# The entry of a hybrid trunk's feed-forward blocks, written out step by step

## The chip, the cores and the metric

One Trainium2 chip, one core. The metric is the device time of one execution of the whole program in microseconds (us); the profile is one such execution. Engines are named as in the profile: PE (matrix multiplication), PEld (its weight load), DVE (vector engine), ACT (activation engine), POOL (GpSimd), SP (the queue that issues most DMAs). DVE, ACT, POOL and SP each take their instructions in the order in which they were issued.

## The reference, cut to what matters

The program computes one inference step of a two-layer trunk on 640 rows (128 context rows and 512 latent rows) of 1024 values: layer 0 mixes tokens by differential attention, layer 1 by a gated linear recurrence, and each is followed by a feed-forward block. What matters here is the step from the mixer's output to the first feed-forward product:

```
xp = xp + mp[2] * op                # residual add, gated; the same for xs
xp = xp + mp[5] * swiglu(adanorm(xp, g_norm_ffn[i], mp[3], mp[4]), w_ffn_in[i], w_ffn_out[i])

adanorm(x, g, shift, scale) = rmsnorm(x, g) * (1.0 + scale) + shift
swiglu(h, w_in, w_out)      = (silu(gate) * up) @ w_out     # gate, up = halves of h @ w_in
```

## The kernel before, in words

Rows lie in five tiles of 128 (t = 0 to 4, `NT`); the feed-forward block takes them as two halves of 320 columns (`HTOK`), so tile 2 lies in both halves. A product in float32 is made of three in a shorter type: each operand is split into a rounded part (`hi`, by ACT) and the rest (`lo`, a subtraction on DVE or POOL), and hi\*hi, hi\*lo and lo\*hi are summed in PSUM. The input product of the feed-forward block runs as a scheme of seven block products (`ffn_in`), except for the first two column groups (`WHOLE`), which are done as plain products by `whole_in` while the sums of blocks that the scheme needs (`sums`) are still being made.

The function `out_and_ffn` holds the entry, once per layer. For each row tile t:

- `last_head(t)` multiplies the last head into the left half of the output projection, and `add_rows` scales the result by the gate and adds it to the residual row (`rtmp`, then `orow`, both on DVE).
- `row_sums(t)` are 24 products (8 steps of 3) for the right half; `close_rows` does the gated add for it (two DVE instructions, the second adds the old row `xc`) and then `unit_rows`: two squares with sums on ACT, three small POOL instructions that make the scale `rs`, and two scaled copies on ACT into `xr`.
- `to_rows(t, eng)` brings the normalised row into the block: eight transposes on PE from `xr` into two PSUM tiles `ntp` (tag `tp`, only two buffers), then for each half of four: a multiplication on DVE into `Hf`, an addition on POOL in place, a rounded copy on ACT (`A1hi`, or `Thi` and `A2hi` for the second half of the columns) and a subtraction on DVE (`A1lo`, `Tlo`, `A2lo`). Half 0 goes through all four before half 1 is multiplied.
- `whole_weights(f, lo_eng)` loads the weights of a column group into two buffers `wr` (three buffers in all) and splits them: `wh` on ACT, `wl` on POOL in three pieces (group 0) or on DVE (group 1).

From `traced["order"] = True` to `traced["order"] = False` the instructions of DVE, ACT and POOL stay in the order of the program; PE does so while `pe["strict"]` holds; SP's loads do so throughout. Outside of that the scheduler chooses. In layer 0 the entry and the block also carry `fill`: a generator of steps (`take(fill)`) that compute the modulation vectors of later layers, each from two weight tiles `raw` loaded by SP and four small products `psada` on PE.

Of the kernel before, what the change touches and what calls it, by code (L numbers as in the profile page):

```python
# [21 lines left out]
P = 128  # L22
# [37 lines left out]
def trunk_kernel(ctx: ExitStack, tc: tile.TileContext, I, O):  # L60
# [91 lines left out]
    def drain(gen):  # L152
        for _ in gen:
            pass

    def take(gen, n=1):
        for _ in range(n):
            next(gen, None)


    def load_raw(src, dims, slots=None):
        tag, n = next(slots) if slots else ("wr", 3)
        r = wp.tile([P, 1024], F32, name="wr", tag=tag, bufs=n)
        n = int(np.prod(dims))
        v = r[:, :n]
        if len(dims) == 2:
            v = v.rearrange("p (a b) -> p a b", a=dims[0])
        elif len(dims) == 3:
            v = v.rearrange("p (a b c) -> p a b c", a=dims[0], b=dims[1])
        if len(dims) < 3:  # L170
            load(out=v, in_=src)
        elif dims[0] <= dims[1]:
            for a in range(dims[0]):
                load(out=v[:, a], in_=src[:, a])
        else:
            for b in range(dims[1]):
                load(out=v[:, :, b], in_=src[:, :, b])
        return r[:, :n]
# [13 lines left out]
        return out  # L192

    def load_split(src, dims, lo_eng, ordered=False, slots=None):
        r = load_raw(src, dims, slots)
# [1055 lines left out]
    def out_and_ffn(l, oT, w_o, open_rows, gcol, xs, reg, xload):  # L1251
        with ExitStack() as sc:
# [67 lines left out]
            def split_rows(dst, src):  # L1320
                AC.activation(dst[0], src, AF.Copy)
                VE.tensor_tensor(dst[1], src, dst[0], ALU.subtract)

            def to_rows(t, eng):
                g = 0 if t == 0 else 1
                row = xr.pop(t)
                c0, c1 = t * P, min((t + 1) * P, HTOK)
                d0, d1 = max(t * P - HTOK, 0), (t + 1) * P - HTOK
                tps = [turn_x(row, hf) for hf in range(2)]
                halves = [slice(4 * hf, 4 * hf + 4) for hf in range(2)]  # L1330
                for ks, tp in zip(halves, tps):
                    ha = Hf[:, ks, t * P : (t + 1) * P]
                    a, b = (adaC[:, l, w, g, ks].unsqueeze(2).to_broadcast([P, 4, P]) for w in (3, 2))
                    VE.tensor_tensor(ha, tp, a, ALU.mult)
                    eng.tensor_tensor(ha, ha, b, ALU.add)
                    if c0 < c1:
                        split_rows([v[:, ks, c0:c1] for v in A1], Hf[:, ks, c0:c1])
                if d0 < d1:
                    split_rows([v[:, 3, :, d0:d1] for v in S], Hf[:, 0:4, HTOK + d0 : HTOK + d1])
                    split_rows([v[:, :, d0:d1] for v in A22], Hf[:, 4:8, HTOK + d0 : HTOK + d1])  # L1340

            def sums(t):
                c0, c1 = max(t * P - HTOK, 0), (t + 1) * P - HTOK
# [16 lines left out]
            def whole_weights(f, lo_eng):  # L1360
                return [
                    load_split(wi[:, 4 * c : 4 * c + 4, :, f * P : (f + 1) * P], [4, 2, P], lo_eng)
                    for c in range(2)
                ]

            def whole_in(ch, half):
                pss = []
# [111 lines left out]
            def last_head(t):  # L1479
                ps = mm_tile([P, 512], "psr")  # L1480
                drain(row_products(ps, oT, w_o[0], range(H - 1, H), t))
                add_rows(ps, t, 0, gates[0])

            def row_sums(t):
                ps = mm_tile([P, 512], "psr")
# [11 lines left out]
            def close_rows(t, ps, xc):  # L1497
                VE.tensor_tensor(xs[t][:, 512:], ps, gates[1][0 if t == 0 else 1], ALU.mult)
                VE.tensor_tensor(xs[t][:, 512:], xs[t][:, 512:], xc, ALU.add)
                xr[t] = unit_rows(t)  # L1500

            def load_xc(t):
                xc = half_tile("xc")
                nc.sync.dma_start(out=xc, in_=xload(t)[:, 512:])
                return xc

            traced["order"] = True
            for t in range(2):
                last_head(t)
                xc = load_xc(t)  # L1510
                drain(sums_[t][1])
                close_rows(t, sums_[t][0], xc)
            for t in range(2, NT):
                last_head(t)
# [20 lines left out]
            for gi, (f0, f1) in enumerate(FF_GROUPS):  # L1535
                nk = f1 - f0
                if gi == 0:
                    to_rows(NT - 2, PO)
                    first.append(whole_weights(1, VE))
                    sums(2)  # L1540
                    sums(3)
                    take(fill)
                    gus = [whole_in(first[0], 0)]
                    take(fill)
                    to_rows(NT - 1, PO)
                    pe["strict"] = False
# [12 lines left out]
                else:  # L1559
                    open_group(nk)  # L1560
# [168 lines left out]
```

## Time and profile before

| what | us |
|---|---|
| median of three runs (1901.63 to 1903.33) | 1902.78 |
| the profiled execution, its own time | 1901.95 |
| its span in the trace | 1900.1 |
| PE busy in the span | 1806.0 |
| DVE, POOL, ACT busy | 1210.7, 894.7, 807.9 |

The profiled execution is 0.8 us shorter than the median. PE is busy for 95% of the span. The entry of layer 0 lies at about 405 to 500 us of the span, that of layer 1 at about 1402 to 1500 us. In the answers that list instructions a line gives the start in us, the length in us, the engine, the operation with its result and its operands, how many were merged, and in brackets how long the engine had been idle before it and on what it had waited last.

### The profile page before, as it was taken

Reading aid. Unit: us, or ns where it says so; the run is one execution under the profiler, and the core shown is the slowest. Engines: PE = TensorE matmul, PEld = TensorE weight load, DVE = VectorE, ACT = ScalarE, POOL = GpSimd, SP = SyncE. Lnnn points to the kernel's source line nnn. Section 1 sums busy time; section 2 is a strip of 40 time slices with the busy share of each in tenths; the row PEclk is TensorE's granted clock in tenths of the full one; section 3 lists DMA queues with packets and bytes.
Section 4 is the critical chain, followed back from the end, with each engine's and each line's share of the span. In section 5 each row is a group of like instructions: output and inputs, shape, how many; then the busy total and the mean of one; then the engine's idle time right before and its main releaser. Section 6 shows DMA issues by size and latency. Waiting matters only on the chain.

```text
span 1900.1 us, 35139 instructions
## 1 busy us (share of the span) xinstructions
PE 1806.0 (95%) x13759; PEld 1615.4 (85%) x13759; DVE 1210.7 (64%) x1997; ACT 807.9 (43%) x1767; POOL 894.7 (47%) x932
## 2 busy tenths in 40 slices
PE   7999999996999999999999999999987999999997
PEld 5799999775878686898889999999877899998996
DVE  4888887745644444476677666666746665656666
ACT  3566666534424232343543333333334433533443
POOL 3345444323462525267227555555424474575562
PEclk9999999998999999999999999999998999999999
DMA  9512211642465554334332222211231233333331
GB/s 314 162 43 67 60 42 59 202 146 64 144 193 163 173 168 150 122 95 128 111 103 82 60 62 63 62 58 61 80 98 38 78 100 100 96 99 101 99 106 67
DMA packets 228239, 200.57 MB, mean 106 GB/s; under 512 B 11566, under 2 KB 177880, under 8 KB 228073
## 3 DMA queue, kind: packets, MB, share of 16 engines
q1 hardware_dynamic: 227266, 197.73, 33.2%
q8 instruction: 108, 1.77, 0.4%
q10 hardware_dynamic: 806, 0.60, 0.1%
q14 instruction: 59, 0.48, 0.1%
HBM read 190.90 MB, written 7.37 MB: 104 GB/s over the span
## 4 chain that ended last, share of the span: by engine, by line
PE 76%; DVE 10%; DMA 4%; issue 3%; ACT 3%; POOL 3%; SPq 0%; POOLq 0%; DVEq 0%; ACTq 0%
PE psr L96 16%; PE psgu L96 15%; PE psqkv L96 8%; PE psf L96 8%; PE psu L96 7%; PE psvg L96 5%; PE psg L96 3%; PE psada L96 3%; PE pso L96 2%; PE S L96 2%; DVE wl L51 2%; PE pa L96 2%; PE po L96 1%; DVE Q L51 1%; DVE orow L51 1%
## 5 line engine op out<-in xcount | busy, mean ns | idle before, releaser
L51 ACT ACTIVATE wh<-wr 128x1024 fp32r<-128x1024 f32 (+2 forms) x224 | 208.1, 937 | 316.9 <-PE psgu L96 143.6
L51 DVE TENSOR_TENSOR wl<-wr,wh 128x1024 fp32r<-128x1024 f32 (+2 forms) x146 | 184.1, 1266 | 202.8 <-ACT wh L51 200.8
L51 POOL TENSOR_TENSOR wl<-wr,wh 128x341 fp32r<-128x341 f32 (+2 forms) x234 | 217.0, 957 | 168.1 <-ACT wh L51 167.6
L96 PE MATMUL psr<-wh,gT 128*128 128x512 f32 (+1 forms) x888 | 286.7, 394 | 2.2 <-DVE gT L51 1.7
L96 PEld LDWEIGHTS psr<-wh,gT 128*128 128x128 f32 x888 | 165.4, 189 | 49.6 <-issue 8.2
L51 POOL TENSOR_TENSOR xr<-wr 128x512 f32<-128x512 f32 x80 | 121.1, 1515 | 136.6 <-DMA wr<-w_ffn_in 135.5
L51 DVE TENSOR_TENSOR wl<-xr,wh 128x1024 fp32r<-128x1024 f32 x80 | 124.7, 1560 | 94.5 <-ACT wh L51 94.2
L96 PE MATMUL psr<-wl,gT 128*128 128x512 f32 (+1 forms) x444 | 173.5, 391 | 0.0
L51 POOL TENSOR_TENSOR u<-u,p 128x320 f32<-128x320 f32 x40 | 57.6, 1441 | 230.3 <-ACT u L51 230.3
L51 POOL TENSOR_TENSOR orow<-orow,rtmp 128x512 f32<-128x512 f32 x100 | 151.2, 1538 | 26.0 <-DVE rtmp L51 26.0
L51 DVE TENSOR_TENSOR rtmp<-psr,gate 128x512 f32<-128x512 f32 (+1 forms) x131 | 85.5, 679 | 66.6 <-PE psr L96 27.0
L51 POOL TENSOR_TENSOR xr<-wr,xr 128x512 f32<-128x512 f32 x80 | 120.0, 1501 | 15.1 <-DVE wl L51 12.7
L96 PE MATMUL psf<-Thi,wh 128*128 128x320 f32 x384 | 123.7, 322 | 2.9 <-DVE gt L51 2.9
L51 ACT ACTIVATE wh<-xr 128x1024 fp32r<-128x1024 f32 x80 | 84.5, 1059 | 90.3 <-PE psgu L96 46.4
L96 PE MATMUL psgu<-Thi,wh 128*128 128x320 f32 x352 | 110.7, 318 | 11.6 <-ACT p L51 6.0
L96 PE MATMUL psf<-Thi,wl 128*128 128x320 f32 x384 | 118.9, 310 | 0.0
L96 PE MATMUL psf<-Tlo,wh 128*128 128x320 f32 x384 | 118.8, 309 | 0.0
L96 PE MATMUL psqkv<-wh,Thi 128*128 128x384 f32 x320 | 109.2, 357 | 1.4 <-ACT Thi L51 1.4
L96 PE MATMUL psgu<-Tlo,wh 128*128 128x320 f32 x352 | 110.2, 313 | 0.0
L96 PE MATMUL psgu<-Thi,wl 128*128 128x320 f32 x352 | 110.0, 313 | 0.0
L96 PE MATMUL psqkv<-wh,Tlo 128*128 128x384 f32 x320 | 104.5, 340 | 0.5 <-DVE Tlo L51 0.5
L96 PE MATMUL psqkv<-wl,Thi 128*128 128x384 f32 x320 | 103.8, 339 | 0.0
(283 smaller groups left out, 5326.9 us busy)
## 6 DMA issues: line engine op xcount, KB each, us to landing
wr<-w_ffn_in SPq DMA_DIRECT2D x176, 256.0 KB
raw<-w_ada SPq DMA_DIRECT2D x112, 256.0 KB
wr<-w_ffn_out SPq DMA_DIRECT2D x40, 512.0 KB
wr<-w_in_rec SPq DMA_DIRECT2D x64, 256.0 KB
gate<-gdram SPq DMA_DIRECT2D x56, 256.0 KB
wr<-w_qkv_attn SPq DMA_DIRECT2D x64, 192.0 KB
ar<-w_ada SPq DMA_DIRECT2D x24, 512.0 KB
wr<-w_ada SPq DMA_DIRECT2D x16, 512.0 KB
```

Source lines behind the costliest of these rows:

```text
L51: ins = op(*a, **k)
L96: in_order(nc.tensor.matmul(*a, **k))
```

## The change: the entry written out

`to_rows` is taken apart into `turn_rows` (the transposes), `modulate` (multiply both halves, then add to both), and `early_blocks`, `late_blocks` with `hi_of` and `lo_of` (round both, subtract both). The loops of the entry are replaced by a list of calls. The raw weights of group 0 are loaded by a call at the top, those of group 1 before the first `modulate`; their splits are calls of their own. For tiles 3 and 4 `add_rows` follows after the products of all heads, and tile 0 is turned after 3 of the 8 steps of `row_sums(2)` instead of 8. The additions of tile 2 move from POOL to DVE. In layer 0 the first three `take(fill)` are gone; one is put ahead of each `put_gT(group, f, 1, ...)`.

```diff
-            def to_rows(t, eng):
...
-                for ks, tp in zip(halves, tps):
-                    ha = Hf[:, ks, t * P : (t + 1) * P]
-                    a, b = (adaC[:, l, w, g, ks].unsqueeze(2).to_broadcast([P, 4, P]) for w in (3, 2))
-                    VE.tensor_tensor(ha, tp, a, ALU.mult)
-                    eng.tensor_tensor(ha, ha, b, ALU.add)
-                    if c0 < c1:
-                        split_rows([v[:, ks, c0:c1] for v in A1], Hf[:, ks, c0:c1])
...
+            def turn_rows(t):
+                row = xr.pop(t)
+                turned[t] = [turn_x(row, hf) for hf in range(2)]
+
+            def modulate(t, eng):
...
+                for ha, tp, c in zip(has, turned.pop(t), a):
+                    VE.tensor_tensor(ha, tp, c, ALU.mult)
+                for ha, c in zip(has, b):
+                    eng.tensor_tensor(ha, ha, c, ALU.add)
...
+            def hi_of(blocks):
+                for dst, src in blocks:
+                    AC.activation(dst[0], src, AF.Copy)
+
+            def lo_of(blocks):
+                for dst, src in blocks:
+                    VE.tensor_tensor(dst[1], src, dst[0], ALU.subtract)
...
-            for t in range(2, NT):
-                last_head(t)
-            first = [whole_weights(0, PO)]
-            for t in range(2, NT):
-                xc = load_xc(t)
-                ps, products = row_sums(t)
-                take(products, (8, 5, 3)[t - 2])
-                to_rows(t - 2, PO)
-                drain(products)
-                close_rows(t, ps, xc)
+            first[0].append(split_raw(w0[0], PO))
+            add_rows(last_head(2), 2, 0, gates[0])
+            pss = [last_head(t) for t in range(3, NT)]
+            xc = load_xc(2)
+            ps2, products = row_sums(2)
+            take(products, 3)
+            turn_rows(0)
+            for ps, t in zip(pss, range(3, NT)):
+                add_rows(ps, t, 0, gates[0])
+            first[0].append(split_raw(w0[1], PO))
+            w1 = whole_weights(1)
+            modulate(0, PO)
+            hi_of(early_blocks(0))
+            take(products, 4)
+            turn_rows(1)
+            drain(products)
+            close_rows(2, ps2, xc)
+            xc = load_xc(3)
+            modulate(1, PO)
+            lo_of(early_blocks(0))
+            hi_of(early_blocks(1))
+            lo_of(early_blocks(1))
+            ps3, products = row_sums(3)
+            drain(products)
+            close_rows(3, ps3, xc)
+            xc = load_xc(4)
+            ps4, products = row_sums(4)
+            take(products, 2)
+            turn_rows(2)
+            modulate(2, VE)
+            hi_of(early_blocks(2))
+            lo_of(early_blocks(2))
+            drain(products)
+            hi_of(late_blocks(2))
+            close_rows(4, ps4, xc)
+            lo_of(late_blocks(2))
...
-                    to_rows(NT - 2, PO)
-                    first.append(whole_weights(1, VE))
+                    turn_rows(3)
+                    modulate(3, PO)
+                    first.append([split_raw(w, VE) for w in w1])
+                    hi_of(late_blocks(3))
+                    lo_of(late_blocks(3))
                     sums(2)
                     sums(3)
-                    take(fill)
                     gus = [whole_in(first[0], 0)]
-                    take(fill)
-                    to_rows(NT - 1, PO)
-                    pe["strict"] = False
+                    turn_rows(4)
+                    modulate(4, PO)
+                    hi_of(late_blocks(4))
+                    lo_of(late_blocks(4))
                     sums(4)
                     weights = ffn_weights(WHOLE)
                     traced["order"] = False
+                    pe["strict"] = False
                     gus.append(whole_in(first[1], 0))
-                    take(fill)
                     open_group(nk)
...
                     for f in range(WHOLE):
+                        take(fill)
                         put_gT(group, f, 1, whole_in(first[f], 1))
                         take(fill)
```

How the instructions stand, DVE at the entry of layer 1, in the kernel before (from the multiplication of tile 0; `orow` is the gated add of a row's right half):

```order
L51 TENSOR_TENSOR Hf<-ntp,adaC 128x4x128
L51 TENSOR_TENSOR A1lo<-Hf,A1hi 128x4x128
L51 TENSOR_TENSOR Hf<-ntp,adaC 128x4x128
L51 TENSOR_TENSOR A1lo<-Hf,A1hi 128x4x128
L51 TENSOR_TENSOR orow<-psr,gate 128x512
L51 TENSOR_TENSOR orow<-orow,xc 128x512
L51 TENSOR_TENSOR Hf<-ntp,adaC 128x4x128
```

The same place in the changed kernel:

```order
L51 TENSOR_TENSOR Hf<-ntp,adaC 128x4x128 x2
L51 TENSOR_TENSOR orow<-psr,gate 128x512
L51 TENSOR_TENSOR orow<-orow,xc 128x512
L51 TENSOR_TENSOR Hf<-ntp,adaC 128x4x128 x2
L51 TENSOR_TENSOR A1lo<-Hf,A1hi 128x4x128 x4
L51 TENSOR_TENSOR orow<-psr,gate 128x512
L51 TENSOR_TENSOR orow<-orow,xc 128x512
```

The subtractions `A1lo` of tiles 0 and 1 moved behind the multiplications of both tiles and behind the closing of tile 2.

ACT, between the scaled copies of tile 4 and the block sums (the same in both layers), as one piece of the difference; `wh` are the rounded weights of group 1, `Thi` and `A2hi` the rounded blocks of tile 3:

```order
 L51 ACTIVATE xr,nss<-orow 128x512 x2
 L51 ACTIVATE xr<-orow,rs 128x512 x2
+L51 ACTIVATE wh<-wr 128x1024 x2
 L51 ACTIVATE Thi<-Hf 128x4x128
 L51 ACTIVATE A2hi<-Hf 128x4x128
-L51 ACTIVATE wh<-wr 128x1024 x2
 L51 ACTIVATE Thi<-Hf 128x8x64
```

The two weight roundings moved ahead of the blocks of tile 3. ACT's other rows of the entry and POOL's, except for the two additions of tile 2, stand as before.

PE in layer 0, behind the 48 products of the first `whole_in` (`psgu`), before:

```order
L96 MATMUL psgu<-A1lo,wh 128x320
L96 MATMUL psgu<-A1hi,wl 128x320
L96 MATMUL psada<-raw,cT 32x256 x2
L96 MATMUL psgu<-A1hi,wh 128x320
L96 MATMUL psgu<-A1lo,wh 128x320
```

and now:

```order
L96 MATMUL psgu<-A1lo,wh 128x320
L96 MATMUL psgu<-A1hi,wl 128x320
L99 MATMUL ntp<-ident,xr 128x128 x8
L96 MATMUL psgu<-A1hi,wh 128x320
L96 MATMUL psgu<-A1lo,wh 128x320
```

The transposes of tile 4 stand directly behind the first `whole_in`, and the first `psada` stands some 95 products later. SP's order in the entry of layer 1 is unchanged; in that of layer 0 it is so up to the eighth `wr<-w_ffn_in` behind the rows `xc`, where four loads of `raw` now follow in place of eight.

## Rows read from the trace of the kernel before

**Rows 1.** PE's waits in 368 to 520 us (layer 0): for what, us, times, longest.

```profile
PE psada L96 <- DMA raw<-w_ada: 9.4, 2, 8.7
PE ntp L99 <- DVE Hf L51: 8.9, 3, 5.5
```

**Rows 2.** PE's waits in 1340 to 1520 us (layer 1), the same columns.

```profile
PE ntp L99 <- DVE Hf L51: 8.9, 3, 5.6
PE psgu L96 <- ACT Thi L51: 5.2, 1, 5.2
PE psgu L96 <- ACT p L51: 3.3, 1, 3.3
```

**Rows 3.** Timeline of PE, layer 1: start, length, instruction, idle before.

```profile
1405.08 0.47 PE L96 MATMUL psr<-wh,Thi 128*128 128x512 f32 x1
...
1415.40 1.04 PE L99 MATMUL ntp<-ident,xr 128*128 128x128 f32 x8
...
1425.86 1.09 PE L99 MATMUL ntp<-ident,xr 128*128 128x128 f32 x4 [5.56 <-DVE Hf L51]
...
1444.08 0.62 PE L96 MATMUL psgu<-A1hi,wh 128*128 128x320 f32 x1
...
1452.27 1.03 PE L99 MATMUL ntp<-ident,xr 128*128 128x128 f32 x8
...
1465.99 1.44 PE L96 MATMUL psgu<-Thi,wh 128*128 128x320 f32 x4 [5.17 <-ACT Thi L51]
```

**Rows 4.** Timeline of POOL, layer 1.

```profile
1417.46 5.27 POOL L51 TENSOR_TENSOR wl<-wr,wh 128x341 fp32r<-128x341 f32 x6 [2.40 <-ACT wh L51]
...
1422.69 1.03 POOL L51 TENSOR_TENSOR Hf<-Hf,adaC 128x512 f32<-128x512 f32 x1
```

**Rows 5.** Timeline of ACT, layer 1.

```profile
1412.36 0.61 ACT L51 ACTIVATE xr<-orow 128x512 f32<-128x512 f32 x1
...
1415.10 1.34 ACT L51 ACTIVATE xr<-orow,rs 128x512 f32<-128x512 f32 x2 [1.42 <-POOL rs L51]
...
1416.34 1.99 ACT L51 ACTIVATE wh<-wr 128x1024 fp32r<-128x1024 f32 x2
...
1426.86 0.63 ACT L51 ACTIVATE A1hi<-Hf 128x512 fp32r<-128x512 f32 x1 [2.48 <-POOL Hf L51]
...
1431.52 1.33 ACT L51 ACTIVATE xr<-orow,rs 128x512 f32<-128x512 f32 x2 [1.21 <-POOL rs L51]
```

**Rows 6.** Timeline of DVE, layer 1.

```profile
1416.04 0.69 DVE L51 TENSOR_TENSOR Hf<-ntp,adaC 128x512 f32<-128x512 f32 x1 [0.61 <-PE ntp L99]
...
1424.42 0.69 DVE L51 TENSOR_TENSOR A1lo<-Hf,A1hi 128x512 fp32r<-128x512 f32 x1 [7.69 <-ACT A1hi L51]
...
1428.85 0.69 DVE L51 TENSOR_TENSOR orow<-orow,xc 128x512 f32<-128x512 f32 x1
...
1452.84 2.35 DVE L51 TENSOR_TENSOR wl<-wr,wh 128x1024 fp32r<-128x1024 f32 x2
...
1455.12 0.87 DVE L51 TENSOR_TENSOR Hf<-Hf 128x256 f32<-128x256 f32 x2
```

**Rows 7.** Timeline of DVE, layer 0.

```profile
418.96 0.69 DVE L51 TENSOR_TENSOR Hf<-ntp,adaC 128x512 f32<-128x512 f32 x1 [0.61 <-PE ntp L99]
...
458.03 0.87 DVE L51 TENSOR_TENSOR Hf<-Hf 128x256 f32<-128x256 f32 x2
...
471.38 1.29 DVE L51 TENSOR_TENSOR Hf<-ntp,adaC 128x512 f32<-128x512 f32 x2 [4.97 <-PE ntp L99]
```

**Rows 8.** Timelines of PE and of SP's queue, layer 0.

```profile
464.23 1.07 PE L96 MATMUL psada<-raw,cT 128*32 128x256 f32 x4 [8.73 <-DMA raw<-w_ada]
...
459.09 18.91 SPq L91 DMA_DIRECT2D raw<-w_ada  x8
```

**Rows 9.** Timeline of POOL, layer 1, later: the first column differences of weights.

```profile
1471.80 3.99 POOL L51 TENSOR_TENSOR xr<-wr 128x512 f32<-128x512 f32 x2
...
1509.77 1.38 POOL L51 TENSOR_TENSOR xr<-wr 128x512 f32<-128x512 f32 x1 [5.96 <-DMA wr<-w_ffn_in]
```

More of the change, by code (lines that the diff above doesn't have):

```diff
@@ L194, in load_split, with split_raw @@
     def load_split(src, dims, lo_eng, ordered=False, slots=None):
-        r = load_raw(src, dims, slots)
+        return split_raw(load_raw(src, dims, slots), lo_eng, ordered)
+    def split_raw(r, lo_eng, ordered=False):
         n = r.shape[1]
@@ L1322, in split_rows @@
                 VE.tensor_tensor(dst[1], src, dst[0], ALU.subtract)
-            def to_rows(t, eng):
-                g = 0 if t == 0 else 1
-                row = xr.pop(t)
-                c0, c1 = t * P, min((t + 1) * P, HTOK)
-                d0, d1 = max(t * P - HTOK, 0), (t + 1) * P - HTOK
-                tps = [turn_x(row, hf) for hf in range(2)]
-                halves = [slice(4 * hf, 4 * hf + 4) for hf in range(2)]
-                for ks, tp in zip(halves, tps):
-                    ha = Hf[:, ks, t * P : (t + 1) * P]
-                    a, b = (adaC[:, l, w, g, ks].unsqueeze(2).to_broadcast([P, 4, P]) for w in (3, 2))
-                    VE.tensor_tensor(ha, tp, a, ALU.mult)
-                    eng.tensor_tensor(ha, ha, b, ALU.add)
-                    if c0 < c1:
-                        split_rows([v[:, ks, c0:c1] for v in A1], Hf[:, ks, c0:c1])
-                if d0 < d1:
-                    split_rows([v[:, 3, :, d0:d1] for v in S], Hf[:, 0:4, HTOK + d0 : HTOK + d1])
-                    split_rows([v[:, :, d0:d1] for v in A22], Hf[:, 4:8, HTOK + d0 : HTOK + d1])
+            HALVES = [slice(4 * hf, 4 * hf + 4) for hf in range(2)]
@@ new lines, in out_and_ffn @@
+            turned = {}
+            def turn_rows(t):
+                row = xr.pop(t)
+                turned[t] = [turn_x(row, hf) for hf in range(2)]
+            def modulate(t, eng):
+                g = 0 if t == 0 else 1
+                has = [Hf[:, ks, t * P : (t + 1) * P] for ks in HALVES]
+                a, b = ([adaC[:, l, w, g, ks].unsqueeze(2).to_broadcast([P, 4, P]) for ks in HALVES] for w in (3, 2))
+                for ha, tp, c in zip(has, turned.pop(t), a):
+                    VE.tensor_tensor(ha, tp, c, ALU.mult)
+                for ha, c in zip(has, b):
+                    eng.tensor_tensor(ha, ha, c, ALU.add)
@@ new lines, in early_blocks, with late_blocks @@
+            def early_blocks(t):
+                c0, c1 = t * P, min((t + 1) * P, HTOK)
+                return [([v[:, ks, c0:c1] for v in A1], Hf[:, ks, c0:c1]) for ks in HALVES] if c0 < c1 else []
+            def late_blocks(t):
+                c0, c1 = max(t * P - HTOK, 0), (t + 1) * P - HTOK
+                if c0 >= c1:
+                    return []
+                dsts = [v[:, 3, :, c0:c1] for v in S], [v[:, :, c0:c1] for v in A22]
+                return [(dst, Hf[:, ks, HTOK + c0 : HTOK + c1]) for dst, ks in zip(dsts, HALVES)]
@@ L1358, in put_late_sums @@
                     split_rows([v[:, 3, :, c0:c1] for v in S], s4)
[L1360 to L1364, printed above, removed]
             def whole_in(ch, half):
@@ L1481, in last_head @@
                 drain(row_products(ps, oT, w_o[0], range(H - 1, H), t))
-                add_rows(ps, t, 0, gates[0])
+                return ps
             def row_sums(t):
@@ L1505, in load_xc, with whole_weights @@
                 return xc
+            def whole_weights(f):
+                return [load_raw(wi[:, 4 * c : 4 * c + 4, :, f * P : (f + 1) * P], [4, 2, P]) for c in range(2)]
             traced["order"] = True
+            w0 = whole_weights(0)
+            first = [[]]
             for t in range(2):
-                last_head(t)
+                ps = last_head(t)
                 xc = load_xc(t)
                 drain(sums_[t][1])
+                add_rows(ps, t, 0, gates[0])
                 close_rows(t, sums_[t][0], xc)
-            for t in range(2, NT):
-                last_head(t)
-            first = [whole_weights(0, PO)]
-            for t in range(2, NT):
-                xc = load_xc(t)
-                ps, products = row_sums(t)
-                take(products, (8, 5, 3)[t - 2])
-                to_rows(t - 2, PO)
-                drain(products)
-                close_rows(t, ps, xc)
+            first[0].append(split_raw(w0[0], PO))
[6 more added lines that the diff above has]
+            for ps, t in zip(pss, range(3, NT)):
+                add_rows(ps, t, 0, gates[0])
+            first[0].append(split_raw(w0[1], PO))
[25 more added lines that the diff above has]
+            lo_of(late_blocks(2))
             fill = iter(())
```

## The prediction

> **What bounds the kernel now.** I first read PE's waits, since PE is busy for 95% of the span: outside the two entries they are short, inside they are the largest of the trace. In layer 1 PE waits 8.9 us in three pieces before transposes, because DVE has not yet emptied the two `ntp` buffers, 5.2 us for the rounded blocks `Thi` of tile 4, and 3.3 us for an eviction `p` at the start of the first `ffn_in` [rows 2]. In layer 0 it waits the same 8.9 us, and 9.4 us for `raw`, the weights of a `fill` step, 8.7 of them in one piece [rows 1, 8]. So the question is what those waits hang on. The timelines say: on a chain that hardly touches PE. POOL makes `wl` of group 0 in six pieces, from 1417.46 to 1422.73, and only then adds to the first half of tile 0 [rows 4]; DVE meanwhile sits idle 7.69 us before the first `A1lo` [rows 6], and since the multiplication of half 1 stands behind that `A1lo`, PE's second four transposes of tile 1 wait 5.56 us [rows 3]. After that the same round (DVE, POOL, ACT, DVE) goes on tile by tile, with the closing of the next tile in its middle, up to the block sums (first `Hf<-Hf` on DVE, 1455.12) [rows 6]. From these on DVE has almost no gaps until the `p` of the first `ffn_in`.
>
> **Two identical layers.** The first multiplication of tile 0 is at 418.96 in layer 0 and 1416.04 in layer 1, a distance of 997.08; the block sums start at 458.03 and 1455.12, a distance of 997.09 [rows 6, 7]. So I work out layer 1 and carry it over; only what comes behind the sums differs. All times below are on layer 1's clock.
>
> **What the change does to the chain.** It removes no instruction of the entry but reorders DVE and PE; ACT and POOL keep their rows, save for the additions of tile 2 and one swap on ACT. The start of the chain therefore stays: tile 1 closes before the split as it does now, ACT rounds `wr` at 1416.34 [rows 5], POOL ends `wl` at 1422.73. I put 0.3 us on top for DVE work that now runs beside it, so 1423.0. From there, with the durations of the rows:
> - POOL adds both halves of tile 0 without a gap, since both are multiplied: 2 x 1.03 gives 1425.1 [rows 4]. ACT rounds the second, 0.63: 1425.7 [rows 5].
> - ACT stands in order, so the squares of tile 2 come only now. From the first square to the first scaled copy is 15.10 - 12.36 = 2.74 us, the two copies 1.34 [rows 5]: `xr` of tile 2 is there at 1429.8.
> - POOL, free of `rs` at 1428.4, adds tile 1: 1430.5; ACT rounds, 0.63: 1431.1; DVE subtracts, 0.69: 1431.8; DVE closes tile 3 with two instructions of 0.69: 1433.2.
> - From the end of such a closing to the first copy is 1431.52 - 1429.54 = 1.98 us [rows 5, 6]: 1435.2, and 1436.5 with the copies. ACT and DVE then finish the early half of tile 2 (half-wide instructions, together 1.0, an estimate from half of 0.63 and of 0.69): 1437.5. Here the first `whole_in` can start on PE; now it starts at 1444.08 [rows 3].
> - DVE closes tile 4: 1438.9; its late half of tile 2 and the multiplications of tile 3, 0.7 and 1.4: 1441.0. ACT copies tile 4 from 1440.9 to 1442.2, rounds the weights, 1.99 [rows 5]: 1444.2, and then tile 3, 2 x 0.63: 1445.5. DVE's two `wl` take 2.35 [rows 6], the second from 1444.2: 1445.4; the two subtractions of tile 3, 1.4: 1446.9.
>
> The block sums start at 1446.9 in place of 1455.12, which is **8.2 us earlier**. What follows (sums, tile 4, `Thi`) has the same rows on DVE, ACT and POOL, so PE's second half of `whole_in` starts at 1457.8 in place of 1465.99 [rows 3], provided PE is done with the two first halves: 1437.5, twice 8.19 (48 products, 1444.08 to 1452.27 [rows 3]) and the transposes give about 1454.9. It is, and waits some 3 us still.
>
> **What PE still waits for.** PE's transposes of tile 0 come after 30 products in place of 45; at 10.32 / 45 = 0.229 us each [rows 3] that is 1412.0, just when `xr` of tile 0 is made, ahead of ACT's square at 1412.36 [rows 5], so that costs at most 0.5. `ntp` is then emptied at once and the three waits of 8.9 us in all go [rows 2]. What is late next is `xr` of tile 2: PE has done 12 products, the transposes of tile 1 and 33 products by about 1425 and stands until 1429.8, close to 5 us. That wait is new, but it lies inside the chain above and is not added to it.
>
> **Behind the sums, layer 0.** There the multiplication of tile 4 waits 4.97 us for PE's transposes [rows 7], because these stand behind a `psada` that waited 8.73 us for `raw` [rows 8]. The changed order on PE puts them ahead of every `fill` step, as in layer 1, where no such wait is. So layer 0 gains 8.2 + 5.0 = **13.2 us**. The `raw` loads sit on SP behind eight weight loads, the last of which waits for `wl` of group 1; that ends at 1445.4 - 997.1 = 448.3, against 458.0 now (1452.84 + 2.35 - 997.1 = 458.1) [rows 6], so `raw` is issued about 449 in place of 459.09 [rows 8] while its first use on PE moves behind two `whole_in`, to about 468. Landing takes about 5 us (459.09 to 464.23 [rows 8]): it is covered by some 14 us.
>
> **The parts with small or no price.** Loading `w0` at the top issues nothing new, since SP's order in the entry is as before: 0; if it delayed `xc` of tile 2, used at about 1419, it would cost what it is late. The swap on ACT is inside the sum. The two additions of tile 2 on DVE cost 1.4 us there, in a stretch where DVE waits for ACT's rounding of tile 2: 0, at worst 1.4 per layer. One `fill` step less before the first `ffn_in` only moves it: 0, or its own 1 us [rows 8]. At the start of `ffn_in`, DVE's `p` and ACT's eviction for it no longer stand behind a `gT`; that may shorten the 3.3 us [rows 2] by up to 1.6 in each layer, and I take 0, since DVE's `wl` there is no earlier than the chain.
>
> **The sum.** 13.2 + 8.2 = 21.4 us off the profiled 1901.95 gives 1880.6; the median stands 0.8 above that execution, so **1881.4, rounded to 1881**.
>
> **Where the Trainium skill speaks against it.** POOL ran two weight differences at 3.99 / 2 = 2.00 us each while DVE was at work, and a like one at 1.38 later [rows 9]. The Trainium skill (GPSIMD Engine Reference, Specifications) says that GpSimd shares its SBUF interfaces with VectorE, with contention from DVE instructions that have two SBUF inputs. The trace agrees by these two rows. By that rule the new DVE work beside `wl` would slow the chain's first link; the price, from rows, is the second rival.
>
> **The rivals.**
> - *All waits go.* If the chain has slack that I don't see, the three longest waits of layer 1 and the two of layer 0 vanish: 17.4 + 18.3 = 35.7 us [rows 1, 2], giving 1867. Against it: ACT still runs the squares of tile 2 behind tile 0's rounding. 12%.
> - *POOL slows beside DVE.* If `wl` stretches as 2.00 to 1.38, 5.27 becomes 7.6, 2.4 us per layer, 4.8 in all: 1886. Of DVE's instructions in that stretch only one of four reads two SBUF tiles, which is why I took 0.3. 16%.
> - *It does not do what it says.* If the second round keeps the sums where they are because tile 4's closing, not tile 0's, sets them, then only the 5 us of layer 0 are left: 1898. The row at 1428.85 speaks against it, since the closing stands late only because of the `A1lo` before it. 5%.
> - *Slower: `fill` starves in layer 0.* The steps shift by one slot through the whole layer and the scheduler there lays PE out anew. Each late `raw` can cost what one cost in the entry, 8.73 us [rows 8]. It decides at the third: three take 26.2 and leave 1881 + 26 = 1907. For it: the loads share SP with the weights. Against it: the loads are issued about 10 us earlier, and each step's weights are asked for one step ahead. 5%.
>
> **How the numbers follow.** My forecast has 62%. Its own range is 1873 to 1889: down by 3.2 (both `p`) and a part of the waits after it, up by 2.8 for tile 2's additions, 0.6 for tile 0's transposes and some latency per link. With the rivals on both sides, 1866 to 1891 leaves out about 2 in 10. What this kernel's measurement can tell from no change is 0.2%, or 3.8 us. Faster: 62 + 12 + 16 + 3 of the third rival = 93%, less 2 for overlooked mishaps, 91%; the same 3%; slower 6%.
>
> **What would show it.** Right: in both layers the block sums start about 31 us after the first multiplication of tile 0 in place of 39.1 (1455.12 - 1416.04); DVE's idle time before the first `A1lo` is spent on tile 1 and the closing of tile 2; PE's waits for `Hf` at `ntp` are nearly gone and one of about 5 us for `xr` stands there; no 8.73 us wait for `raw` in layer 0. Wrong: PE still waiting for `Thi` as long before and the sums at 39 us; a `wl` group on POOL well above 5.3 us; new waits for `raw` after 500 us; or PE without any wait in the entry, which would mean that the chain was not the bound.

## The result and the profile after

| | median us | range us | runs |
|---|---|---|---|
| before | 1902.2 | 1898.9 to 1903.3 | 4 |
| changed | 1886.3 | 1885.1 to 1889.8 | 4 |

The ratio is 0.9922, with a 95% interval of 0.9904 to 0.9941: 15.9 us faster where 21.4 were forecast, and inside the range of 1866 to 1891. The profiled execution took 1889.76 us, its span is 1887.9. It is 3.5 us above the median, and it lost as much ahead of every changed instruction: at 65 us PE's granted clock fell to 0.50 after a wait for modulation weights (last section), and layer 0's entry begins 4.13 us later than in the trace of before (first `rtmp` of tile 0 on DVE at 413.11 against 408.98). Times of layer 0 below are given with these 4.13 taken off, called *adjusted*; layer 1's entry begins 2.14 us earlier than before's, and there 2.14 is added.

PE's waits around the entry of layer 1, in the changed kernel (what PE waited for, us, times, longest):

```profile
PE psgu L96 <- ACT Thi L51: 5.4, 1, 5.4
PE ntp L99 <- ACT xr L51: 5.1, 2, 4.2
PE psgu L96 <- ACT p L51: 1.8, 1, 1.8
...
PE ntp L99 <- DVE Hf L51: 0.3, 1, 0.3
```

Beside [rows 2], the 8.9 us for `Hf` are down to 0.3, the wait for `xr` of tile 2 has come in their place, the one for `Thi` is as long as it was, and the one for `p` has lost 1.5. In layer 0 the wait of 8.7 us for `raw` [rows 1] is gone (372 to 525 us):

```profile
PE psada L96 <- DMA raw<-w_ada: 0.5, 2, 0.2
```

PE's timeline in layer 1 shows where the waits stand (start, length, instruction, idle time before it and what ended it):

```profile
1414.05 1.23 PE L99 MATMUL ntp<-ident,xr 128*128 128x128 f32 x8 [0.28 <-DVE Hf L51]
1427.00 1.97 PE L99 MATMUL ntp<-ident,xr 128*128 128x128 f32 x8 [4.23 <-ACT xr L51]
...
1456.35 1.43 PE L96 MATMUL psgu<-Thi,wh 128*128 128x320 f32 x4 [5.38 <-ACT Thi L51]
```

The last row answers to 1465.99 of [rows 3]: adjusted 1458.49, 7.5 us earlier. DVE, the same stretch:

```profile
1413.22 1.28 DVE L51 TENSOR_TENSOR Hf<-ntp,adaC 128x512 f32<-128x512 f32 x2
...
1417.62 1.28 DVE L51 TENSOR_TENSOR Hf<-ntp,adaC 128x512 f32<-128x512 f32 x2
1422.82 1.69 DVE L51 TENSOR_TENSOR A1lo<-Hf,A1hi 128x512 fp32r<-128x512 f32 x2 [3.93 <-ACT A1hi L51]
...
1432.02 1.28 DVE L51 TENSOR_TENSOR Hf<-Hf,adaC 128x512 f32<-128x512 f32 x2
...
1445.49 0.88 DVE L51 TENSOR_TENSOR Hf<-Hf 128x256 f32<-128x256 f32 x2
```

Tile 1 is multiplied before the first `A1lo`, whose wait is 3.93 us in place of 7.69. From the first multiplication to the block sums it is 32.27 us in place of 39.08 [rows 6]; in layer 0 it is 32.23 (422.41 to 454.64). POOL, where the chain begins:

```profile
1415.33 5.80 POOL L51 TENSOR_TENSOR wl<-wr,wh 128x341 fp32r<-128x341 f32 x6 [2.40 <-PE ntp L99]
1421.08 2.04 POOL L51 TENSOR_TENSOR Hf<-Hf,adaC 128x512 f32<-128x512 f32 x2
...
1425.36 0.19 POOL L51 TENSOR_SCALAR ms<-nss 128x1 f32<-128x1 f32 x1
1425.64 0.55 POOL L51 TENSOR_TENSOR rs<-ms,mhalf 128x1 f32<-128x1 f32 x1
...
1432.02 0.74 POOL L51 TENSOR_SCALAR ms<-nss 128x1 f32<-128x1 f32 x1
1432.84 0.88 POOL L51 TENSOR_TENSOR rs<-ms,mhalf 128x1 f32<-128x1 f32 x1
```

`wl` takes 5.80 us where it took 5.27 [rows 4], and the two small instructions of tile 3 take 1.6 us together where those of tile 2 take 0.7: they run at 1432.02, beside DVE's additions of tile 2.

**Where the rest went.** I follow one instruction of each `ffn_in` of layer 0 on DVE (`u<-u,psu`). In the changed kernel:

```profile
501.74 0.48 DVE L51 TENSOR_TENSOR u<-u,psu 128x320 f32<-128x320 f32 x1
518.23 0.48 DVE L51 TENSOR_TENSOR u<-u,psu 128x320 f32<-128x320 f32 x1
578.96 0.49 DVE L51 TENSOR_TENSOR u<-u,psu 128x320 f32<-128x320 f32 x1 [0.55 <-PE psu L96]
...
934.79 0.48 DVE L51 TENSOR_TENSOR u<-u,psu 128x320 f32<-128x320 f32 x1
```

and in the kernel before:

```profile
511.03 0.48 DVE L51 TENSOR_TENSOR u<-u,psu 128x320 f32<-128x320 f32 x1
530.31 0.47 DVE L51 TENSOR_TENSOR u<-u,psu 128x320 f32<-128x320 f32 x1
576.71 0.48 DVE L51 TENSOR_TENSOR u<-u,psu 128x320 f32<-128x320 f32 x1
...
936.59 0.48 DVE L51 TENSOR_TENSOR u<-u,psu 128x320 f32<-128x320 f32 x1
```

The first comes 9.29 us earlier (adjusted 13.4), the second 12.08, the third 2.25 later. Between the second and the third, where the first `rows_out` stands (the output product of the first group of columns), 14.3 us are lost; the expectations below call this stretch that between the third and fourth `ffn_in`. About 4 come back later, for a reason that was not followed up: at the last of the 20 rows the lead is 1.80, adjusted 5.9. PE at the first `rows_out`, in the changed kernel:

```profile
521.30 0.50 PE L96 MATMUL psr<-wh,gT 128*128 128x512 f32 x1 [1.68 <-ACT gT L51]
523.77 0.73 PE L96 MATMUL psr<-wh,gT 128*128 128x512 f32 x2 [1.27 <-DVE gT L51]
528.05 1.07 PE L96 MATMUL psada<-raw,cT 128*32 128x256 f32 x4 [3.54 <-DMA raw<-w_ada]
```

and the load it waits for on SP's queue:

```profile
522.90 7.05 SPq L91 DMA_DIRECT2D raw<-w_ada  x6
```

The busy times by stretch of 10 us (PE, PEld, DVE, ACT, POOL, granted clock, DMA share, GB/s), changed kernel:

```profile
515.00:525.00 10.00, 6.55 (x38) 5.33 (x36) 7.12 (x10) 4.23 (x7) 3.87 (x4) 1.00 0.48 137
525.00:535.00 10.00, 6.95 (x23) 4.82 (x23) 1.29 (x3) 0.00 (x0) 3.88 (x4) 0.66 0.52 179
```

and before, where PE has no gap at all:

```profile
515.00:525.00 10.00, 10.00 (x62) 7.74 (x61) 3.00 (x4) 3.56 (x8) 1.30 (x1) 1.00 0.48 141
525.00:535.00 10.00, 10.00 (x58) 9.16 (x58) 6.16 (x8) 4.55 (x8) 6.42 (x5) 1.00 0.34 100
```

The order of PE tells why. Before, 11 `fill` steps stand ahead of the first `rows_out`: a set of modulation vectors (ten steps, the first of which only loads) ends in them, the loads of the next set are asked for, its first products stand ahead of the last `psu` (519.19), and behind that `psu` come 45 `psr` in a row. The changed kernel has 10. The set still ends there, but the next set's first products stand 6 `psr` behind the last `psu`, and their `raw` is asked for at 522.90 only, behind six weight loads. The other traces say the same. In every kernel with 10 steps ahead (the changed one and, of those below, fill_minus, l0_only, lo_inline, w1_after, tile2_pool, wl_late), 11.2 to 14.8 us are lost in this stretch and PE waits 3.5 to 5.1 us for `raw` (fill_held, which moves later steps too: 8.1 and 3.1); in every one with 11 (fill_plus, l1_only, fill_wait, wl_late_wait, steps_behind) no more than about 1 us is lost, and that wait is 0.3 us or less.

### The profile page after: what moved, and what is told of

Its sections match the earlier page's. It is cut to its first block, busy times and chain, and to the rows that moved or that the text cites. A ratio compares the mean times of both kernels' runs of the same rounds, so it can differ in the third digit from the quotient of the medians.

```text
span 1887.9 us, 35138 instructions
## 1 busy us (share of the span) xinstructions
PE 1804.6 (96%) x13759; PEld 1612.6 (85%) x13759; DVE 1210.9 (64%) x2001; ACT 807.9 (43%) x1767; POOL 890.9 (47%) x928
## 4 chain that ended last, share of the span: by engine, by line
PE 75%; DVE 9%; POOL 4%; DMA 4%; issue 4%; ACT 3%; SPq 0%; POOLq 0%; DVEq 0%; ACTq 0%
PE psr L96 16%; PE psgu L96 14%; PE psqkv L96 8%; PE psf L96 8%; PE psu L96 7%; PE psvg L96 5%; PE psg L96 3%; PE psada L96 2%; PE pso L96 2%; PE S L96 2%; DVE wl L51 2%; PE pa L96 2%; PE po L96 1%; DVE Q L51 1%; POOL wl L51 1%
## 5 line engine op out<-in xcount | busy, mean ns | idle before, releaser
L96 PE MATMUL psgu<-Thi,wh 128*128 128x320 f32 x352 | 111.7, 320 | 14.8 <-ACT Thi L51 10.8
```

What stands on the lines that cost most here:

```text
L96: in_order(nc.tensor.matmul(*a, **k))
```

## The experiments

Theory A: the chain through POOL, ACT and DVE sets the end of the entry, the change shortened it about as worked out, and what is missing was lost to the moved `fill` step in layer 0. Rival B: POOL's slowing beside DVE took it, in both entries alike. Rivals C and D are named where they are tested. Each group of kernels has its own runs of the kernel before, and the ratio goes by these. Where two kernels of different groups are compared, the difference of their ratios (the changed kernel has 0.9922) stands beside that of their medians: the two can be 3 to 4 us apart.

| kernel | us | ratio to before, 95% interval |
|---|---|---|
| fill_plus | 1882.8 | 0.9886, 0.9865 to 0.9907 |
| fill_minus | 1907.2 | 1.0019, 1.0008 to 1.0031 |
| l1_only | 1889.9 | 0.9932, 0.9909 to 0.9954 |
| l0_only | 1896.0 | 0.9966, 0.9950 to 0.9983 |
| lo_inline | 1895.8 | 0.9970, 0.9954 to 0.9986 |
| w1_after | 1888.1 | 0.9920, 0.9892 to 0.9948 |
| tile2_pool | 1884.1 | 0.9901, 0.9873 to 0.9929 |
| wl_late | 1875.9 | 0.9849, 0.9815 to 0.9883 |
| fill_wait | 1882.1 | 0.9883, 0.9865 to 0.9901 |
| fill_held | 1881.6 | 0.9884, 0.9870 to 0.9898 |
| wl_late_wait | 1869.2 | 0.9824, 0.9810 to 0.9838 |
| steps_behind | 1900.1 | 0.9985, 0.9970 to 0.9999 |

**The step that was dropped, put back (fill_plus) and taken from the kernel before (fill_minus).** On the changed kernel:

```diff
                         take(fill)
+                    take(fill)
                     put_late_sums()
```

> The changed kernel with one more fill step (a product of the modulation weights) directly behind the second put_gT of the entry in layer 0, so that 11 steps in place of 10 stand ahead of the first rows_out, as in the kernel before. Theory A (the engine chain gained what was forecast, and the step that was dropped costs about 7 us between the third and fourth ffn_in of layer 0): PE's order in the first rows_out is again the old one, the waits there for raw and gT go, time 1879 to 1881 against 1886. Rival B (POOL beside DVE in the entries took the missing gain): the entries are the same, so the time stays at 1886, plus or minus 1.

On the kernel before:

```diff
                     gus.append(whole_in(first[1], 0))
-                    take(fill)
                     open_group(nk)
```

> The kernel before with its third fill step of layer 0's entry left out at that place (the steps themselves are all done, one slot later), nothing else: 10 in place of 11 steps ahead of the first rows_out. Theory A: this alone loses what the changed kernel loses there, about 7 us: 1909 against 1902. Rival B: a step that moves costs nothing: 1902, plus or minus 1.5.

fill_minus lost 0.19%, about 4 us by the runs. Its trace loses 14.8 us between the second and the third `ffn_in` of layer 0 and is 6.1 behind at the end of the layer, in a kernel whose entry is otherwise as before. PE there, the same two rows as in the changed kernel:

```profile
529.29 0.50 PE L96 MATMUL psr<-wh,gT 128*128 128x512 f32 x1 [1.68 <-ACT gT L51]
...
536.27 1.07 PE L96 MATMUL psada<-raw,cT 128*32 128x256 f32 x4 [4.86 <-DMA raw<-w_ada]
```

fill_plus has no such loss: 1.0 us between those two `ffn_in`. It gains 3.5 us by the medians, less than expected, and 6.8 by the ratios. It has a late `raw` of its own, 2.2 us at 492 us, with PE's clock at 0.73 in the 5 us from 491, and its lead at the first `ffn_in` is 10.0 us (adjusted by the 3.33 that its own entry begins later) where the changed kernel has 13.4. Rival B expected no change from either kernel, and falls as the main cause; the size is 4 to 7 us by the times.

**One layer at a time (l1_only, l0_only).** Old entry and new in one kernel:

```diff
+            NEW = l == 1
+            if NEW:
+                w0 = whole_weights(0)
...
+            else:
+                for t in range(2):
+                    old_head(t)
```

> The new entry in layer 1 alone, the old one in layer 0. Theory A (layer 1 gains all of the chain, about 10 us; layer 0 gains 13 and loses 7 again in its first rows_out): 1892. Rival B (contention in both entries takes the missing gain alike, so that each has half of 16): 1894. If only layer 0's wait for raw counted: 1902. A and B are told apart more by the trace: in A the block sums of layer 1 stand 31 to 32 us behind the first multiplication of tile 0, and layer 0 is as before.

> The new entry in layer 0 alone (with its order of the fill steps), the old one in layer 1. Theory A: 13 us ahead at the first ffn_in, 6 ahead at the end of layer 0: 1896. Rival B: 1894, and no loss between the third and fourth ffn_in. With layer 1 alone the two gains should add up to the 16 us of the whole change, within 1.5.

Layer 1 alone gives 12.9 us by its ratio, layer 0 alone 6.5. The sum of 19.4 misses the 16 within 1.5 that I expected; the ratios' intervals are 3 to 4 us wide to either side, so it does not disagree with 15.9 either. Rival B wanted equal halves; the traces decide: in l1_only the sums stand 32.3 us behind the first multiplication in layer 1 and 39.1 in layer 0. In l0_only the lead of layer 0 goes from 13.0 us at the second `ffn_in` to 1.3 behind at the third (not adjusted; its entry begins 2.67 later than that of before), and PE waits 4.7 us for `raw` there.

**DVE's order alone undone (lo_inline).**

```diff
+            def old_modulate(t, eng):
...
+                for ks, tp, blk in zip(HALVES, turned.pop(t), early_blocks(t)):
...
+                    VE.tensor_tensor(ha, tp, a, ALU.mult)
+                    eng.tensor_tensor(ha, ha, b, ALU.add)
+                    hi_of([blk])
+                    lo_of([blk])
...
-            modulate(0, PO)
-            hi_of(early_blocks(0))
+            old_modulate(0, PO)
...
-            modulate(1, PO)
-            lo_of(early_blocks(0))
-            hi_of(early_blocks(1))
-            lo_of(early_blocks(1))
+            old_modulate(1, PO)
```

> The changed kernel with tiles 0 and 1 handled half by half again (multiply, add, round, subtract of half 0 before the multiplication of half 1), all else as changed. Theory A (the order multiply both, then the rest, on DVE is what shortens the chain): PE's waits for Hf at ntp come back (5 to 6 us in each layer), the block sums start 36 to 39 us behind the first multiplication of tile 0 in place of 32.2, and the time is 1894 to 1898. Rival C (the gain is that of the swap on ACT, the early loads and the order on PE): sums stay near 32 us, time 1886 to 1888.

The old wait is back, in one piece of 9.0 us in each layer (I had put 5 to 6 on it). This is layer 1, the wait and DVE's first multiplication and first block sum:

```profile
PE ntp L99 <- DVE Hf L51: 9.3, 2, 9.0
...
1410.56 0.68 DVE L51 TENSOR_TENSOR Hf<-ntp,adaC 128x512 f32<-128x512 f32 x1
...
1448.43 0.87 DVE L51 TENSOR_TENSOR Hf<-Hf 128x256 f32<-128x256 f32 x2
```

The sums stand 37.9 us behind the first multiplication in both layers: 5.6 of the 6.8 us that the change took out of this stretch are DVE's order for tiles 0 and 1. 9.5 us are lost by the medians, 9.1 by the ratios. Theory A as expected in the sums and the time; rival C (the swap, the loads, PE's order) is left with the other 1.2.

**The swap on ACT undone (w1_after) and tile 2 on POOL again (tile2_pool).**

```diff
-                    first.append([split_raw(w, VE) for w in w1])
                     hi_of(late_blocks(3))
                     lo_of(late_blocks(3))
+                    first.append([split_raw(w, VE) for w in w1])
```

> The changed kernel with the split of the weights of group 1 behind the rounding and subtracting of tile 3, as before. Theory A: the swap only changes the order at the chain's end; the blocks of tile 3 come 2 us earlier, wl ends later, the sums move by at most 1 us per layer: 1885 to 1888. Rival C: half of the gain or more goes: 1893 or later.

```diff
-            modulate(2, VE)
+            modulate(2, PO)
```

> The changed kernel with the two additions of tile 2 on POOL again. Their 1.28 us leaves DVE, and POOL's rs of tile 3, which took 0.74 and 0.88 us beside them in place of 0.19 and 0.55, should be back at these. Theory A: POOL's two additions take 2.0 us where DVE's took 1.3, so the blocks of tile 2 come about 0.7 later while xr of tile 3 comes 0.9 earlier: sums at 31.3 to 32.5 us, 1885 to 1887. Rival B (contention is what eats the gain): sums 1 us earlier or more in each layer, 1884 or less.

The swap is worth nothing: 1888.1 and sums at 32.20. With tile 2 on POOL the two small instructions of tile 3 are back at 0.19 and 0.55, and the sums come at 31.85, 0.4 earlier:

```profile
1429.95 0.19 POOL L51 TENSOR_SCALAR ms<-nss 128x1 f32<-128x1 f32 x1
1430.22 0.55 POOL L51 TENSOR_TENSOR rs<-ms,mhalf 128x1 f32<-128x1 f32 x1
```

So rival B's mechanism exists, and taking it away is worth 0.4 us per layer here; the 2.2 us between the medians (4.0 between the ratios) are within the spread of the runs.

**POOL's differences out of the chain (wl_late).** The rounding of `w0` stays, POOL's six `wl` go behind `rs` of tile 3, and the loads of group 1 with them:

```diff
-            first[0].append(split_raw(w0[0], PO))
+            his = [split_hi(w0[0])]
...
-            first[0].append(split_raw(w0[1], PO))
-            w1 = whole_weights(1)
+            his.append(split_hi(w0[1]))
...
             close_rows(3, ps3, xc)
             xc = load_xc(4)
+            first[0] = [split_lo(r, hi) for r, hi in zip(w0, his)]
+            w1 = whole_weights(1)
```

> The changed kernel with POOL's six differences wl of group 0 (5.8 us) moved from ahead of the additions of tile 0 to behind rs of tile 3; their rounding on ACT stays. Theory A (the chain through POOL sets the end of the entry): xr of tile 2 comes 5 us earlier, PE's wait for it (4.2) goes, the block sums start 27 to 28.5 us behind the first multiplication in place of 32.2, PE's wait for Thi falls from 5.4 to under 2, and the time is 1875 to 1879. Rival D (DVE and ACT, not POOL, set the end): sums stay within 1 us of 32.2, 1885 to 1887. Against A: rs of tile 4 then stands behind wl, and the weights of group 1 get their slots later; if that decides, 1883 or later.

1875.9 us, 10.4 below the changed kernel (13.9 by the ratios). POOL adds to tile 0 at once, and DVE's sums stand 28.27 us behind the first multiplication in place of 32.27:

```profile
1410.24 2.04 POOL L51 TENSOR_TENSOR Hf<-Hf,adaC 128x512 f32<-128x512 f32 x2 [1.04 <-DVE Hf L51]
...
1424.27 6.10 POOL L51 TENSOR_TENSOR wl<-wr,wh 128x341 fp32r<-128x341 f32 x6
...
1409.48 1.28 DVE L51 TENSOR_TENSOR Hf<-ntp,adaC 128x512 f32<-128x512 f32 x2
...
1437.75 0.88 DVE L51 TENSOR_TENSOR Hf<-Hf 128x256 f32<-128x256 f32 x2
```

The chain is the bound, and POOL was its first link. PE's wait for `xr` of tile 2 is gone, as expected. Not as expected, the one for `Thi` grew to 6.30 us: the chain reaches `Thi` 4.0 us sooner after the first multiplication, but PE arrives 4.9 sooner:

```profile
1418.91 1.03 PE L99 MATMUL ntp<-ident,xr 128*128 128x128 f32 x8
1425.11 1.27 PE L99 MATMUL ntp<-ident,xr 128*128 128x128 f32 x8 [1.07 <-ACT xr L51]
...
1448.62 1.43 PE L96 MATMUL psgu<-Thi,wh 128*128 128x320 f32 x4 [6.30 <-ACT Thi L51]
```

**Where a `fill` step may stand (fill_wait, fill_held, steps_behind).** fill_wait, on the changed kernel, puts the first step's products into PE's wait for `Thi`. To hold them there it also keeps PE's order strict through the second of the two first halves:

```diff
+                    take(fill)
                     gus = [whole_in(first[0], 0)]
...
+                    gus.append(whole_in(first[1], 0))
+                    take(fill)
                     pe["strict"] = False
-                    gus.append(whole_in(first[1], 0))
...
                     for f in range(WHOLE):
-                        take(fill)
+                        if f:
+                            take(fill)
```

> The changed kernel with 11 fill steps ahead of the first rows_out, as fill_plus, but with the loads of the first asked for ahead of the first whole_in and its products directly behind the two first halves, where PE stands 5.4 us for Thi. Theory A: the first rows_out is as in the kernel before (no loss between the third and fourth ffn_in, against 14 us in the changed kernel), and the step costs nothing since PE waits there anyway; fill_plus's late raw (2.2 us) goes: 1878 to 1881. Rival E (the loads of raw are late wherever the step stands): a wait for raw of 2 us or more in the entry again, 1883 or later.

```profile
458.34 1.09 PE L96 MATMUL psada<-raw,cT 128*32 128x256 f32 x8
463.80 1.43 PE L96 MATMUL psgu<-Thi,wh 128*128 128x320 f32 x4 [4.37 <-ACT Thi L51]
```

The products take 1 us out of a wait that was 5.4, `raw` is there, and the lead in layer 0 holds: 12.5 us at the first `ffn_in` (10.15, and 2.39 for the later start of this execution), 11.9 at the last. By the medians it is 1882.1, 1 to 4 us above what I expected, 4.2 below the changed kernel (7.4 by the ratios); at the end of layer 0 its trace is 5.9 us ahead of that of the changed kernel.

fill_held leaves 10 steps ahead but holds those of tiles 0 and 1 back:

```diff
                         add_rows(ps, t, half, gates, PO if after is None else VE)
-                        take(fill)
+                        if held and t < 2:
+                            continue
+                        take(fill, 3 if held and t == 2 else 1)
```

> The changed kernel with 10 steps ahead of the first rows_out, as it is, but the steps behind its tiles 0 and 1 held back to tile 2. Theory A': the products of the next set, laid early between the psr of the first tiles, are what PE waits at: held back, the wait for raw there (3.5 us) goes, the loss of 14 us between the third and fourth ffn_in falls to about half, 1882 to 1884. Rival F (the set that ends there is asked for too late in any order): the wait stays, 1885 to 1888.

Half right: the wait for `raw` stays (3.1 us), as rival F said, but the loss between the two `ffn_in` falls from 14.3 to 8.1 us, as A' said, and the time is 1881.6. The missing step and the place of the following ones both count, and the one late `raw` is not the whole loss.

steps_behind takes the other term by itself: the kernel before, with its five steps behind both first halves.

```diff
                     sums(3)
-                    take(fill)
                     gus = [whole_in(first[0], 0)]
-                    take(fill)
                     to_rows(NT - 1, PO)
...
                     gus.append(whole_in(first[1], 0))
-                    take(fill)
...
                     for f in range(WHOLE):
+                        take(fill)
                         put_gT(group, f, 1, whole_in(first[f], 1))
                         take(fill)
+                    take(fill)
```

> The kernel before with its five fill steps of layer 0's entry moved behind both first halves (one ahead of each put_gT of the second halves, one behind each, one at the end), so that the transposes of tile 4 no longer stand behind a psada; 11 steps ahead of the first rows_out as before. Theory A: this alone gives the 5.0 us that the prediction put down to the psada at 464 us: the multiplication of tile 4 comes 5 us earlier and the time is 1896 to 1899, with no loss in the first rows_out. Rival G: the step whose raw is late costs as much wherever it stands, since the end of the entry hangs on the sums: 1901 to 1903.

1900.1, 2.9 us less than before: between the two expectations. The 4.97 us of [rows 7] do go, and `p` of the first `ffn_in` comes 5.0 us earlier in this execution's own time. But one of the steps behind has a late `raw` now:

```profile
497.10 0.80 PE L96 MATMUL psada<-raw,cT 128*32 128x256 f32 x4 [3.14 <-DMA raw<-w_ada]
```

and at the first `ffn_in` 2.3 of the 5.0 are left; at the last of the 20 rows the kernel is 1.6 us behind (938.74, 0.55 off for its later entry, against 936.59). That the execution is 3.2 us shorter all the same comes from behind layer 0, from code that is the same: there the granted clock of the kernel before falls to 0.73 in 980 to 985 and 1355 to 1360 us, and here it stays at 1.00. So the 5 us at the multiplication are real, but this trace shows nothing of them at the end of the layer, and the 2.9 us between the medians (interval 0.2 to 5.7) are not shown to come from the entry. In the changed kernel and fill_wait the shorter chain stands beside them; what the 5 us are worth alone stays open.

**Both together (wl_late_wait).** wl_late with the edit of fill_wait.

> wl_late and fill_wait together. If the two causes are separate (the POOL chain in both entries, the fill steps in layer 0), the gains add up: 1876 less 4 to 6 gives 1870 to 1872. If the earlier entry makes raw late again: 1874 to 1876.

1869.2 us, 17.1 below the changed kernel (18.6 by the ratios) and 33 to 34 below the kernel before: the fastest of all, faster than expected by 1. The two gains alone sum to 14.6 by the medians and 21.3 by the ratios, so they add up as well as these runs can tell. The traces are closer: the edit of fill_wait brings 5.9 us at the end of layer 0 on the changed kernel and on wl_late alike. So the causes are separate.

## Why the prediction was right, and which term was not

- *The bound and the chain: right.* The waits for `Hf` went but for 0.3 us, the wait for `xr` of tile 2 came (4.23 us against "close to 5"), the wait for `Thi` stayed. wl_late shows that POOL's `wl` is the first link. The wait for `Thi` is 5.38 us where I had "some 3": the 8.19 us for a first half were read where PE's granted clock was 0.51 at first (1444.0 to 1446.5 us of the kernel before); at 1.00 it takes 7.35 (1435.55 to 1442.90), so PE is there sooner. That lies inside the wait and costs nothing.
- *8.2 us to the block sums: 7.5 measured,* 6.8 in the stretch itself and 0.7 because tile 0 is multiplied sooner. The difference is POOL. `wl` took 0.2 more than I had put on, but the closing of tile 3 ends at 1433.04 (adjusted) where I had 1433.2; it is at `rs` of tile 3 that the chain falls behind, by the 0.9 that POOL's two small instructions take more. The Trainium skill (GPSIMD Engine Reference, Specifications) has contention between GpSimd and VectorE when VectorE's instruction has two SBUF inputs; the trace agrees for the small instructions, 0.19 to 0.74 and 0.55 to 0.88 us beside DVE's additions of tile 2, and tile2_pool takes it away. The rival's price of 2.4 us per layer was too large.
- *13.2 us in layer 0: right up to the first `ffn_in`* (`p` 12.6, `u` 13.4 adjusted).
- *Behind the sums in layer 1 it gained more:* 10.1 us to the end of the span. `p` is 7.9 earlier (8.2 forecast), the other 2 lie behind it, where I had taken 0 and up to 1.6. About half of the 2 is PE's clock and no gain: from `p` to `u` it is 9.81 us before and 7.62 now, but 7.18 (l0_only, the old code) and 6.08 (l1_only, the new) where the clock held, which leaves 1.1 for the change, whose wait for `p` is 1.6 us shorter.
- *The term that was mis-sized: the moved `fill` step,* priced "0, or its own 1 us". In the profile of the changed kernel it cost 13.4 - 5.9 = 7.5 us, in fill_minus 6.1 by its trace and about 4 by the times, and fill_wait brings back 5.9 by its trace and 4 to 7 by the times. My reason was that the loads are asked for a step ahead. They are, but the first loads of a set are asked for by a step of their own; with one step fewer that step falls into `rows_out`, its products land among the first `psr`, and there `raw` comes late. My fourth rival named this mechanism, and I let it count from the third late load. One late load, with the order around it, was enough for a third of the forecast gain; "new waits for `raw` after 500 us" stood among my signs of being wrong, and they came (3.54 us at 528).
- *The sum:* 21.4 less 7.5 in layer 0, plus 2 in layer 1, is 16, as measured. That it meets so closely is partly luck: 1.1 of the 2 is clock, and the step's price is known only as 4 to 7.5. The time lies in my range because the range had room for a term that I had put at nothing.

## What to carry to other kernels

When a long wait goes, the next link is worth looking at before anything else: here it was work on POOL that ended 15 us before PE first used it (1421.1 and 1436.2 us in the changed kernel), and moving it gave as much again as two thirds of the whole change. Background steps that are spread over a schedule have no price of their own, only one by place: put them where the engine stands anyway and where their load has landed, and look again at every place that shifts by one. A change in the count of such steps is to be looked up in the built order, not taken as neutral.

## What the runs showed of the hardware

The same wait can cost more or less, by what PE's clock does behind it. Ahead of the first `ffn_in` of layer 1, PE waits 3.30 us for `p` in the kernel before and 3.29 in l0_only, whose layer 1 is the same code; PE's instructions behind it stand in the same order. The kernel before (columns as above):

```profile
1491.00:1496.00 5.00, 4.21 (x16) 4.21 (x17) 2.63 (x4) 1.75 (x5) 0.00 (x0) 0.50 0.29 105
1496.00:1501.00 5.00, 5.00 (x31) 5.00 (x31) 1.23 (x1) 1.54 (x3) 0.00 (x0) 0.83 0.00 0
```

and l0_only:

```profile
1487.00:1492.00 5.00, 4.13 (x28) 4.13 (x29) 2.86 (x5) 2.89 (x6) 0.00 (x0) 1.00 0.30 105
1492.00:1497.00 5.00, 5.00 (x36) 5.00 (x35) 2.70 (x3) 2.44 (x3) 1.35 (x1) 1.00 0.00 0
```

Granted clock 0.50 (1.2 of 2.4 GHz) and 0.83 against 1.00 and 1.00: from `p` to `u` it is 9.81 us in the one and 7.18 in the other, 2.6 for nothing but the clock. In the changed kernel the clock fell there too (0.66 in 1481 to 1486 us), behind a wait of 1.80. The 4.13 us at the start of the changed kernel's execution are of the same kind. There PE waits 1.96 us for `ar` and then has half its clock:

```profile
60.00:65.00 5.00, 3.04 (x29) 1.99 (x21) 5.00 (x11) 3.45 (x7) 2.04 (x4) 0.97 1.07 311
65.00:70.00 5.00, 5.00 (x21) 3.68 (x22) 2.60 (x6) 2.07 (x5) 2.58 (x4) 0.50 0.58 159
```

In fill_held, the same code up to layer 0, the clock holds there:

```profile
65.00:70.00 5.00, 5.00 (x38) 4.51 (x39) 4.03 (x13) 3.70 (x10) 3.08 (x5) 1.00 0.56 156
```

All 14 traces fall into two groups here, with code that is the same up to layer 0. In seven the clock in 65 to 70 us is 0.50 to 0.66, and layer 0's entry begins 2.4 to 4.1 us later than in the kernel before; in the other seven, the kernel before among them, it is 1.00, and the entries begin within 0.7 us of each other. The length of the wait for `ar` does not tell them apart: 2.01 us kept the clock in wl_late_wait, 1.74 lost it in tile2_pool. So single executions differ by 2 to 4 us through the clock in one place, and a trace can carry a gain or a loss that is not the change's. What decides in one execution that it falls was not tried and stays open.
